# Where the norm's sums, the next weights and the modelled hand-overs stand in three planned feed-forwards

## The chip, the cores and the metric

The kernel runs on one core of a Trainium2 chip. The metric is the time of one execution in microseconds (us) of the device, from which the median of several runs is taken. The core's engines are TensorE (PE in the profile, with its weight loads as PEld), VectorE (DVE), ScalarE (ACT), GpSimd (POOL) and SyncE (SP), which issues most transfers.

## The reference

A decoder trunk of two layers on 512 tokens of width 1024, everything in float32. Cut to what matters:

```
D, F = 1024, 2816
def swiglu_ffn(x, w_gate, w_up, w_down):
    return (jax.nn.silu(x @ w_gate) * (x @ w_up)) @ w_down
for layer in range(2):
    h = h + 0.5 * swiglu_ffn(rms_norm(h, ffn1_norm[layer]), ...)
    u = rms_norm(h, mix_norm[layer])
    h = h + (conformer_conv(u, ...) if layer == 0 else attention(u @ w_q, k_shared, v_shared) @ w_o)
    h = h + 0.5 * swiglu_ffn(rms_norm(h, ffn2_norm[layer]), ...)
    if layer == 0:
        k_shared, v_shared = split(rms_norm(h, kv_norm) @ w_kv)
return rms_norm(h, final_norm)
```

So there are four feed-forwards, each behind an RMS norm, whose factor is one number for each token: the root of the mean square over the 1024 channels.

## The kernel before, in words

**Layout.** Activations stand transposed: 8 chunks of 128 channels by 512 tokens. A weight tile is 128x1024. Each float32 operand is split into a high part (`whi`, `xhi`, `hhi`, made by ScalarE) and the rest (`wlo`, `xlo`, `hlo`, made by VectorE), and a product takes three matmuls: high by high, high by low, low by high (`mm3`, L355 to L357).

**Order of the stages.** Feed-forward 0 and the convolution of layer 0, then feed-forward 1, feed-forward 2, keys, queries and attention, and last feed-forward 3. The first feed-forward is written in program order (`ffn`). Feed-forwards 1, 2 and 3 go through `planned` (L511), and these three are what the change touches.

**The planner.** `planned` writes down every step with an engine, an estimated duration and a rank (`plan.add`), and `Plan.issue` then runs a list scheduling by these numbers: of the steps that can start, it takes the one that can start first, and of those the one of lowest rank. The result is a fixed instruction order for PE, DVE and ACT; each engine works through its own in order. A step that depends on one of another engine is taken to be startable `LATE` = 0.15 us after it, whichever engines they are.

**A feed-forward's start.** The products use `norm.x`, the chunks with the gain but without the norm's factor; the factor is multiplied in when a result leaves PSUM. The factor is made like this: the squares are summed over the chunks into `norm.acc` (VectorE); `token_sums` (L387) adds over the partitions with eight narrow matmuls into the PSUM tile `ss`; `root` takes the inverse root on VectorE in 14 tiny steps (L617 to L621); the result is spread over the partitions by eight diagonal pieces (L628) and two matmuls (L631), and ScalarE copies the row `rb` to SBUF (L633, tile `r_f`). `seed` (L637) writes three PSUM banks that later hold running sums, with any finite matmul of `norm.x[0]`.

**PSUM.** Of eight banks three are these seeds; five go round between `ss`, the row (`pb`) and the products. In a third of the hidden columns the plain columns come first (`plain`, two products of 24 matmuls), and from column 4 on `seven` computes gate and up together by a seven-product scheme, whose products have 12 matmuls of 256 columns each. Between these products stand ScalarE copies of PSUM (`u`, `g1`, `m5`, `u3`; L722 to L730) that the next product waits for. Columns 4 to 21 are of this kind, 18 in each of the three feed-forwards, 54 in all. VectorE prepares sums of `norm.x` for it (`right_sums`, tiles `xs`, `ts`, `tlo`) and of the weights (`st`, `sl`, `wlo`, `ul`).

**Weights.** `unit` hands out the next weight tile and keeps one more loaded ahead, by `load(rank + 0.4)`: transfer, split on ScalarE, split on VectorE, all behind the steps of rank `rank`, the outputs of the running column among them.

Of the kernel before, what the change touches and what calls it, by code (L numbers as in the profile page):

```python
# [15 lines left out]
D = 1024  # L16
# [65 lines left out]

SEVEN = {i: tuple(range(4, 22)) for i in (1, 2, 3)}

DIRECT = 6
Z_BANKS = 4
AV_BANKS = 2
# [3 lines left out]
class Buf:  # L91


    def __init__(self, kind, make):
        self.kind, self.make, self.ap, self.slot = kind, make, None, None
# [7 lines left out]
class Plan:  # L103
# [5 lines left out]
    LATE = 0.15  # L109
    SELF = {"V": 0.14, "A": 0.1, "G": 0.02}  # L110

    def __init__(self, room):
        self.room, self.steps, self.last = dict(room), [], {}

    def add(self, engine, work, do, r=(), w=(), rank=0, port=False):
        n, after = len(self.steps), set()
        for x in r:
            writer, readers = self.last.setdefault(x, [None, []])
            if writer is not None:
                after.add(writer)  # L120
            readers.append(n)
        for x in w:
            writer, readers = self.last.get(x, [None, []])
            after.update(readers)
            if writer is not None:
                after.add(writer)
            self.last[x] = [n, []]
        after.discard(n)
        bufs = tuple(dict.fromkeys(x for x in (*r, *w) if isinstance(x, Buf)))
        self.steps.append((engine, work, do, after, (rank, n), bufs, port or engine == "G"))  # L130
        return n

    def issue(self):
        steps = self.steps
        first, final = {}, {}
        for n, st in enumerate(steps):
            for x in st[5]:
                first.setdefault(x, n)
                final[x] = n
        waits = [len(st[3]) for st in steps]  # L140
        follow = [[] for _ in steps]
        for n, st in enumerate(steps):
            for m in st[3]:
                follow[m].append(n)
        ends, free = [None] * len(steps), {}
        room = {k: list(range(n)) for k, n in self.room.items()}
        ready = {n: 0.0 for n in range(len(steps)) if not waits[n]}
        freeing, uses = [], {}
        for n, st in enumerate(steps):
            for x in st[5]:  # L150
                uses[x] = uses.get(x, 0) + 1
        order, now, port = [], 0.0, (0.0, None)
        while ready or freeing:
            best = None
            for n, t in ready.items():
                engine = steps[n][0]
                t = max(t, free.get(engine, 0.0), now)
                if steps[n][6] and port[1] != engine:
                    t = max(t, port[0])
                new = [x for x in steps[n][5] if first[x] == n]  # L160
                if any(len(room[x.kind]) < sum(y.kind == x.kind for y in new) for x in new):
                    continue
                key = (t, steps[n][4])
                if best is None or key < best[0]:
                    best = (key, n, new)
            if freeing and (best is None or min(freeing)[0] <= best[0][0]):
                t, _, kind, slot = min(freeing)
                freeing.remove(min(freeing))
                room[kind].append(slot)
                now = max(now, t)  # L170
                continue
            assert best is not None, "no step can be issued"
            (t, _), n, new = best
            engine, work, do, _, _, bufs, ported = steps[n]
            for x in new:
                x.slot = room[x.kind].pop(0)
            ends[n] = t + work
            free[engine] = t + work
            if ported:
                port = (t + work, engine)  # L180
            del ready[n]
            order.append((t, n))
            for x in bufs:
                uses[x] -= 1
                if not uses[x]:
                    freeing.append((ends[n] + self.LATE, len(freeing) + len(order), x.kind, x.slot))
            for m in follow[n]:
                waits[m] -= 1
                if not waits[m]:
                    ready[m] = max(  # L190
                        ends[j] + (self.SELF.get(steps[m][0], 0.0) if steps[j][0] == steps[m][0] else self.LATE)
                        for j in steps[m][3]
                    )
        for _, n in order:
            steps[n][2]()
# [3 lines left out]
def decoder_kernel(ctx, tc, xin, gu, dna, dnb, pw1, pw2, kq, wv, wo, out):  # L199
    nc = tc.nc  # L200
    V, A, G, PE = nc.vector, nc.scalar, nc.gpsimd, nc.tensor
# [306 lines left out]
    def planned(idx, norm, after, early=None, sums=None, late=None, tail=None, ahead=1):  # L508


        with ExitStack() as c:  # L511
# [3 lines left out]
            N2 = T // 2  # L515
            seeds = {x: banks[i][:, :N2] for i, x in enumerate(("u0", "u1", "g1"))}
            plan = Plan({"bank": 5, "raw": 3, "whi": 3, "wlo": 3, "wh1": 1, "wl1": 1, "st": 1, "sh": 1, "sl": 1,
                         "uh": 1, "ul": 1, "sq": 2, "m5": 2, "u3": 2, "tg": 2, "tu": 2, "hhi": 8, "hlo": 8, "-": 99})
            add = plan.add
            halves = [slice(0, N2), slice(N2, T)]  # L520

# [10 lines left out]
            def load(rank):  # L532

                src = next(order, None)
                if src is None:
                    return
                i = count[0]
                count[0] += 1
                if isinstance(src, list):
                    held.append(load_seven(i, src, rank))  # L540
                    return
                n = src.shape[-1]
                full = [tile("raw", f"raw{i}", UNIT, F32, wp), tile("whi", f"whi{i}", UNIT, F32R, wp),
                        tile("wlo", f"wlo{i}", UNIT, F32R, wp)]
                add("D", 3.0, lambda: nc.sync.dma_start(full[0]()[:, :n], src), w=[full[0]], rank=rank)
                f = n / UNIT
                add("A", 0.95 * f, lambda: A.copy(full[1]()[:, :n], full[0]()[:, :n]), r=[full[0]], w=[full[1]], rank=rank)  # L547
                add("V", 1.14 * f, lambda: V.tensor_sub(  # L548
                    full[2]()[:, :n], full[0]()[:, :n], full[1]()[:, :n].bitcast(F32)),
                    r=full[:2], w=[full[2]], rank=rank)  # L550
                held.append((full[1], full[2]))
# [48 lines left out]
            def unit(rank):  # L600

                turn[0] += 1
                while len(held) < 2:
                    n = len(held)
                    load(rank + 0.4)
                    if len(held) == n:
                        break
                return held.pop(0)
# [2 lines left out]
            rb = tp.tile([P, T], F32, name=f"r_{norm.name}", tag="r", bufs=1)  # L611
            small, v = (tp.tile([P, 4], F32, name=f"{x}_{norm.name}", tag=x, bufs=1) for x in ("rs", "v"))
            ss, pb, dg = bank(), bank(), []
            add("PE", 0.5, lambda: token_sums(ss()[:, :4], norm.acc), w=[ss], rank=-2)

            def root():
                V.tensor_scalar_add(v, ss()[:, :4], RMS_EPS)  # L617
# [3 lines left out]
                V.tensor_sub(parts[:, 4:], small, parts[:, :4].bitcast(F32))  # L621
                dg.append(parts)

            add("V", 2.4, root, r=[ss], w=["root"], rank=-2)
            for h in range(2):
                dh = tile("sq", f"dg_{norm.name}_{h}", T, F32R, tp)
                for b in range(4):
# [4 lines left out]
                    r=[dh], w=[pb], rank=-2)  # L632
# [1023 lines left out]
```

## Time and profile before

| what | value |
|---|---|
| median of 3 runs | 1917.21 us (1917.21, 1914.41, 1917.89) |
| the profiled execution itself | 1914.83 us |
| its span, first to last instruction | 1913.0 us |
| mean granted clock of TensorE | 0.992 |
| busy: PE, PEld, DVE, ACT, POOL | 1877.6, 1661.9, 1395.3, 956.1, 280.6 us |

The profile counts an engine as busy while an instruction of it runs. The wait rows say which line of which engine stood idle, which instruction's end let it go on, the total time, how often and the longest. The timeline has one row for each instruction: start, duration, engine, line, tiles, and in brackets the idle time before it. Matmuls overlap in the pipeline, so their own durations are longer than the distance from one start to the next, and it is the distance that counts.

The three entries that are spoken of below are the moments at which feed-forwards 1, 2 and 3 begin: near 553, 907 and 1541 us of the span. They are called the first, second and third entry.

### The profile page before, as it was taken

The page shows a single profiled execution, that of the slowest core. Times are in us where ns is not written, and L with a number is a line of the kernel's source. Part 1 is how long each engine was busy: PE and PEld are TensorE (multiplying, and loading weights), DVE is VectorE, ACT ScalarE, POOL GpSimd, SP SyncE. Part 2 cuts the span into 40 slices and gives each one's busy share as a digit, 9 for nine tenths or more (in the row PEclk, how much of TensorE's full clock was granted, in tenths as well). Part 3 has the DMA queues.
Part 4 walks back from the last instruction along what each step waited for, and adds up shares of the span by engine and source line. Part 5 has one row for each costly group of instructions (what it writes and reads, how often), then busy time and mean ns, then how long its engine had stood idle before and what let it go on. Part 6 is the DMA issues. An engine that isn't in the chain of part 4 may idle for free. (4 is left out here: it accounts for less than half of the span.)

```text
span 1913.0 us, 28433 instructions
## 1 busy us (share of the span) xinstructions
PE 1877.6 (98%) x11037; PEld 1661.9 (87%) x11037; DVE 1395.3 (73%) x2295; ACT 956.1 (50%) x1581; POOL 280.6 (15%) x267
## 2 busy tenths in 40 slices
PE   9999999999999999999999999999999999999997
PEld 7888888878988999898798999988888779899896
DVE  6544534598878679577985967878999689577585
ACT  5424324686554345255452544647777645354353
POOL 0311302089700000000000000004543100000001
PEclk9999999999999999999999999999999999999998
DMA  5756746444422323323242232452223122323232
GB/s 202 255 177 236 270 151 216 158 165 156 142 67 89 112 87 100 121 84 115 78 165 78 100 122 89 125 170 74 86 83 83 56 90 97 123 70 130 84 102 70
DMA packets 74262, 237.95 MB, mean 124 GB/s; under 512 B 8464, under 2 KB 11152, under 8 KB 74128
## 3 DMA queue, kind: packets, MB, share of 16 engines
q1 hardware_dynamic: 65776, 209.41, 32.8%
q10 hardware_dynamic: 8352, 26.74, 3.7%
q8 instruction: 86, 1.41, 0.3%
q14 instruction: 48, 0.39, 0.1%
HBM read 200.46 MB, written 31.46 MB: 121 GB/s over the span
## 5 line engine op out<-in xcount | busy, mean ns | idle before, releaser
L249 ACT CAST whi<-raw 128x1024 fp32r<-128x1024 f32 (+3 forms) x109 | 107.5, 989 | 204.0 <-PE pg L356 112.3
L355 PE MATMUL bank<-hhi,whi 128*128 128x512 f32 x510 | 198.5, 389 | 0.0
L356 PE MATMUL bank<-hlo,whi 128*128 128x512 f32 x510 | 198.5, 389 | 0.0
L357 PE MATMUL bank<-hhi,wlo 128*128 128x512 f32 x510 | 198.4, 389 | 0.0
L547 ACT CAST whi<-raw 128x1024 fp32r<-128x1024 f32 (+1 forms) x93 | 92.8, 998 | 191.8 <-PE bank L356 161.8
L505 ACT CAST whi<-raw 128x1024 fp32r<-128x1024 f32 x108 | 113.1, 1048 | 83.9 <-DMA raw<-in_gu_dram 33.9
L250 DVE TENSOR_TENSOR wlo<-raw,whi 128x1024 fp32r<-128x1024 f32 (+3 forms) x109 | 131.2, 1208 | 25.0 <-ACT whi L249 24.7
L357 PE MATMUL pg<-xhi_f,wlo 128*128 128x512 f32 x352 | 137.0, 390 | 0.6 <-DVE wlo L250 0.5
L355 PE MATMUL pg<-xhi_f,whi 128*128 128x512 f32 x352 | 136.3, 390 | 0.8 <-ACT whi L249 0.8
L356 PE MATMUL pg<-xlo_f,whi 128*128 128x512 f32 x352 | 136.9, 389 | 0.0
L801 DVE SCALAR_TENSOR_TENSOR xpar<-bank,xpar 128x512 f32<-128x512 f32 x69 | 47.7, 691 | 122.1 <-PE bank L357 121.5
L506 DVE TENSOR_TENSOR wlo<-raw,whi 128x1024 fp32r<-128x1024 f32 x108 | 131.7, 1220 | 4.1 <-ACT whi L505 4.1
L684 PE MATMUL bank<-thi,whi 128*128 128x256 f32 x432 | 123.3, 285 | 3.2 <-ACT u L730 2.7
L686 PE MATMUL bank<-thi,sl 128*128 128x256 f32 x432 | 122.6, 284 | 1.6 <-DVE sl L506 1.6
L684 PE MATMUL bank<-thi,sh 128*128 128x256 f32 x432 | 122.5, 283 | 0.0
L686 PE MATMUL bank<-xhi_f,wlo 128*128 128x256 f32 x432 | 122.3, 283 | 0.0
L685 PE MATMUL bank<-xlo_f,whi 128*128 128x256 f32 x432 | 122.2, 283 | 0.0
L686 PE MATMUL bank<-thi,wlo 128*128 128x256 f32 x432 | 122.2, 283 | 0.0
L685 PE MATMUL bank<-tlo,sh 128*128 128x256 f32 x432 | 122.2, 283 | 0.0
L685 PE MATMUL bank<-tlo,whi 128*128 128x256 f32 x432 | 122.2, 283 | 0.0
L684 PE MATMUL bank<-xhi_f,whi 128*128 128x256 f32 x432 | 122.2, 283 | 0.0
L548 DVE TENSOR_TENSOR wlo<-raw,whi 128x1024 fp32r<-128x1024 f32 (+1 forms) x93 | 107.2, 1153 | 18.6 <-ACT whi L547 18.5
(400 smaller groups left out, 5713.6 us busy)
## 6 DMA issues: line engine op xcount, KB each, us to landing
raw<-in_gu_dram SPq DMA_DIRECT2D x174, 512.0 KB, 3.3
raw<-in_dna_dram SPq DMA_DIRECT2D x64, 512.0 KB, 3.9
praw<-in_pw_dram SPq DMA_DIRECT2D x24, 512.0 KB, 4.3
aparth<-phi ACTq DMA_DIRECT2D x24, 512.0 KB, 2.6
apartl<-plo ACTq DMA_DIRECT2D x24, 512.0 KB, 3.8
raw<-in_dnb_dram SPq DMA_DIRECT2D x32, 384.0 KB, 3.3
whi<-aparth SPq DMA_DIRECT2D x21, 512.0 KB, 3.3
wlo<-apartl SPq DMA_DIRECT2D x21, 512.0 KB, 4.3
```

The source lines that it names most:

```text
L249: ins = A.copy(dst_hi, src)
L250: (G if on_pool else V).tensor_sub(dst_lo, src, dst_hi.bitcast(F32))
L355: PE.matmul(ps, w[0], x[0], start=first, stop=False)
L356: PE.matmul(ps, w[0], x[1], start=False, stop=False)
L357: PE.matmul(ps, w[1], x[0], start=False, stop=last)
L505: plan.add("A", a, lambda: A.copy(hi(), src()), r=[src, *r], w=[hi], rank=rank)
L506: plan.add("V", v, lambda: V.tensor_sub(lo(), src(), hi().bitcast(F32)), r=[src, hi, *r], w=[lo, *w], rank=rank)
L547: add("A", 0.95 * f, lambda: A.copy(full[1]()[:, :n], full[0]()[:, :n]), r=[full[0]], w=[full[1]], rank=rank)
L548: add("V", 1.14 * f, lambda: V.tensor_sub(full[2]()[:, :n], full[0]()[:, :n], full[1]()[:, :n].bitcast(F32)), r=full[:2], w=[full[2]], ran ...
L684: PE.matmul(d, a[0], b[0], start=start and q == 0, stop=False, skip_group_check=True)
L685: PE.matmul(d, a[0], b[1], start=False, stop=False, skip_group_check=True)
L686: PE.matmul(d, a[1], b[0], start=False, stop=last_, skip_group_check=True)
```

## The change

It has four parts, all of them numbers and steps of the planner; no instruction of an engine is added or taken away.

1. Two steps that issue nothing are put in front: one takes VectorE for 3.5 us of the model, the other (on an engine of its own, "joint") 5.0 us, and `token_sums` depends on the latter. In the model `token_sums` can therefore start no earlier than about 5 us after the feed-forward begins.
2. The estimated duration of `root` goes from 2.4 to 2.9 us.
3. The next weight tile is ranked at `rank - 0.5` in place of `rank + 0.4`, that is ahead of the outputs of the running column. The copies `u` and `g1` have `rank - 1`, and the copy `m5` has `rank - 0.5`.
4. The planner gets a table of hand-over times by the engine that produces (transfer 1.0, PE 0.35, VectorE 0.2, ScalarE 0.2 us) in place of 0.15 for all. Only `planned` uses it.

```
+LAG = {"D": 1.0, "PE": 0.35, "V": 0.2, "A": 0.2, "-": 0.0}
+HEAD = (3.5, 5.0)
...
-    def __init__(self, room):
-        self.room, self.steps, self.last = dict(room), [], {}
+    def __init__(self, room, lag=None):
+        self.room, self.steps, self.last, self.lag = dict(room), [], {}, lag or {}
...
                     ready[m] = max(
-                        ends[j] + (self.SELF.get(steps[m][0], 0.0) if steps[j][0] == steps[m][0] else self.LATE)
+                        ends[j] + (self.SELF.get(steps[m][0], 0.0) if steps[j][0] == steps[m][0]
+                                   else self.lag.get(steps[j][0], self.LATE))
                         for j in steps[m][3]
                     )
...
-                    load(rank + 0.4)
+                    load(rank - 0.5)
...
-            add("PE", 0.5, lambda: token_sums(ss()[:, :4], norm.acc), w=[ss], rank=-2)
+            add("V", HEAD[0], lambda: None, rank=-9)
+            add("joint", HEAD[1], lambda: None, w=["acc_in"], rank=-9)
+            add("PE", 0.5, lambda: token_sums(ss()[:, :4], norm.acc), r=["acc_in"], w=[ss], rank=-2)
...
-            add("V", 2.4, root, r=[ss], w=["root"], rank=-2)
+            add("V", 2.9, root, r=[ss], w=["root"], rank=-2)
```

The lines move by 4 to 6 with it: `token_sums` is L391 after, `mm3` L359 to L361, `seed` L643, the split of a weight on VectorE L552 (L548 before).

The first place is TensorE at the second entry. `bank1_7` is the last output product of feed-forward 1, `acc_f1_1` the sum of squares, `xhi_f1_1_0` the first chunk of the new input. Before:

```order
L355 MATMUL bank1_7_5095<-hhi1_21_8312,whi138_8457 128x512
L356 MATMUL bank1_7_5095<-hlo1_21_8317,whi138_8457 128x512
L357 MATMUL bank1_7_5095<-hhi1_21_8312,wlo138_8464 128x512
L387 MATMUL bank2_3_8570<-onesD_74,acc_f1_1_5081 128x1 x4
L637 MATMUL bank2_0_8567<-xhi_f1_1_0_8336,onesr_72 128x256
L637 MATMUL bank2_1_8568<-xhi_f1_1_0_8336,onesr_72 128x256
L637 MATMUL bank2_2_8569<-xhi_f1_1_0_8336,onesr_72 128x256
L355 MATMUL bank2_4_8571<-xhi_f1_1_0_8336,whi139_8487 128x512
```

After, the same engine at the end of the first product, 21 matmuls of it behind the seeds:

```order
L359 MATMUL bank2_3_8570<-xhi_f1_1_6_8527,whi139_8486 128x512
L360 MATMUL bank2_3_8570<-xlo_f1_1_6_8534,whi139_8486 128x512
L361 MATMUL bank2_3_8570<-xhi_f1_1_6_8527,wlo139_8494 128x512
L391 MATMUL bank2_4_8571<-onesD_74,acc_f1_1_5081 128x1 x4
L359 MATMUL bank2_3_8570<-xhi_f1_1_7_8544,whi139_8486 128x512
L360 MATMUL bank2_3_8570<-xlo_f1_1_7_8548,whi139_8486 128x512
L361 MATMUL bank2_3_8570<-xhi_f1_1_7_8544,wlo139_8494 128x512
L359 MATMUL bank2_5_8572<-xhi_f1_1_0_8341,whi140_8506 128x512
```

The sums moved from the first place of the feed-forward to behind seven eighths of its first product; the seeds are now first. The other two entries read alike, and in all three the matmuls of the row (`pb`) moved from the second product to the third. Apart from these, TensorE's order differs only in a few products that change places with a neighbour.

At the first entry the chunks come in the order 1, 2, 7, 3, 4, 5, 6, 0, so that the seeds, which read chunk 0, read the last one to be made. TensorE there, after (`pp0_1` is the last product of the convolution):

```order
L361 MATMUL pp0_1_5046<-shi7_4483,wlo88_4873 128x256
L643 MATMUL bank1_0_5088<-xhi_f2_0_0_5072,onesr_72 128x256
L643 MATMUL bank1_1_5089<-xhi_f2_0_0_5072,onesr_72 128x256
L643 MATMUL bank1_2_5090<-xhi_f2_0_0_5072,onesr_72 128x256
L359 MATMUL bank1_3_5091<-xhi_f2_0_1_4889,whi89_4878 128x512
```

Here the chunk that was made last is what TensorE meets first; on ScalarE the instruction ahead of that chunk's (the split of weight 91) is the same as before.

The second place is VectorE at the third entry: the split `wlo226` of the second product's weights, and the root of the norm, which begins with `v_f2_1` and ends with `dp_f2_1`. Before:

```order
L620 CAST dp_f2_1_15254<-rs_f2_1_15221 128x4
L621 TENSOR_TENSOR dp_f2_1_15254<-rs_f2_1_15221,dp_f2_1_15254 128x4
L667 TENSOR_TENSOR ts3_0_15270<-xs3_0_15229 128x256
L667 TENSOR_TENSOR ts3_0_15270<-xs3_1_15236,ts3_0_15270 128x256
L548 TENSOR_TENSOR wlo226_15279<-raw226_15231,whi226_15268 128x1024
```

After:

```order
L439 TENSOR_TENSOR acc_f2_1_14819<-acc_f2_1_14819,sq_f2_1_7_15199 128x512
L659 TENSOR_TENSOR xs3_1_15254<-xhi_f2_1_1_15033,xlo_f2_1_1_15034 128x512
L673 TENSOR_TENSOR ts3_0_15259<-xs3_0_15247 128x256
L552 TENSOR_TENSOR wlo226_15261<-raw226_15228,whi226_15252 128x1024
L623 TENSOR_SCALAR v_f2_1_15222<-bank3_4_15216 128x4
L397 TENSOR_SCALAR rs_f2_1_15221<-v_f2_1_15222 128x4
```

The split went from behind the root to ahead of it. Behind the root, `wlo227` and `wlo228` now come before the diagonal pieces.

The third place is ScalarE at the first `seven` of feed-forward 3 (column 4): the copy of `u0` (`bank3_0`), of `m5` and of `g1` (`bank3_2`), between splits of hidden values (`hhi`) and weights (`whi`, `sh`). Before:

```order
L505 CAST whi234_0_15644<-raw234_0_15614 128x1024
L722 COPY bank3_0_15212<-bank3_3_15215 128x256
L505 CAST hhi3_3_15662<-tu3_3_15639 128x512
L725 COPY m5_3_4_15676<-bank3_6_15218 128x256
L726 COPY bank3_2_15214<-bank3_0_15212 128x256
L505 CAST sh234_15695<-st234_15619 128x1024
L730 COPY u3_3_4_15725<-bank3_0_15212 128x256
```

After:

```order
L580 CAST uh233_15614<-raw233_0_15481 128x512
L728 COPY bank3_0_15212<-bank3_4_15216 128x256
L731 COPY m5_3_4_15667<-bank3_7_15219 128x256
L509 CAST hhi3_3_15669<-tu3_3_15637 128x512
L732 COPY bank3_2_15214<-bank3_0_15212 128x256
L509 CAST whi234_0_15689<-raw234_0_15635 128x1024
L509 CAST sh234_15704<-st234_15652 128x1024
```

The split `whi234_0` went from ahead of the copies to behind the copy of `g1`, and `m5` went ahead of `hhi3_3`.

More of the change, by code (lines that the diff above doesn't have):

```diff
@@ L517, in planned @@
             plan = Plan({"bank": 5, "raw": 3, "whi": 3, "wlo": 3, "wh1": 1, "wl1": 1, "st": 1, "sh": 1, "sl": 1,
-                         "uh": 1, "ul": 1, "sq": 2, "m5": 2, "u3": 2, "tg": 2, "tu": 2, "hhi": 8, "hlo": 8, "-": 99})
+                         "uh": 1, "ul": 1, "sq": 2, "m5": 2, "u3": 2, "tg": 2, "tu": 2, "hhi": 8, "hlo": 8, "-": 99}, lag=LAG)
             add = plan.add
```

## The prediction

> **What bounds the kernel now.** I read the busy times first, then TensorE's waits, then the timeline at the places where the long waits stand. The page's first part:
>
> ```profile
> PE 1877.6 (98%) x11037; PEld 1661.9 (87%) x11037; DVE 1395.3 (73%) x2295; ACT 956.1 (50%) x1581; POOL 280.6 (15%) x267
> ```
>
> TensorE is busy for 98% of the span of 1913.0 us, the next engine for 73%. The change leaves TensorE's instructions as they are, so it can only win what TensorE stands idle, 1913.0 − 1877.6 = 35.4 us, and what it runs at a lower clock. TensorE's waits, longest first (line, what ended the wait: total us, times, longest):
>
> ```profile
> PE bank L387 <- DVE acc_f L435: 6.6, 2, 3.5
> PE pb_out1v L1527 <- ACT dg_out L1518: 4.9, 1, 4.9
> PE bank L387 <- DVE acc_f L774: 3.7, 1, 3.7
> PE bank L684 <- ACT u L730: 2.7, 6, 0.8
> PE bank L686 <- DVE sl L506: 1.6, 3, 0.6
> ```
>
> The largest are `token_sums` (L387) waiting for the sum of squares, once at each entry: 6.6 + 3.7 = 10.3 us. L1527 is the end of the kernel, which the change doesn't touch. The last two rows, nine waits and 4.3 us, are hand-overs among the products of `seven`. The second entry on TensorE's timeline:
>
> ```profile
> 894.63 0.39 PE L357 MATMUL bank<-hhi,wlo 128*128 128x512 f32 x1
> ...
> 906.87 0.39 PE L357 MATMUL bank<-hhi,wlo 128*128 128x512 f32 x1
> 910.94 1.84 PE L387 MATMUL bank<-onesD,acc_f 128*128 128x1 f32 x8 [3.69 <-DVE acc_f L774]
> 912.64 0.99 PE L637 MATMUL bank<-xhi_f,onesr 128*128 128x256 f32 x3
> 913.43 0.63 PE L355 MATMUL bank<-xhi_f,whi 128*128 128x512 f32 x1
> ...
> 915.99 0.53 PE L355 MATMUL bank<-xhi_f,whi 128*128 128x512 f32 x1
> 916.36 0.40 PE L356 MATMUL bank<-xlo_f,whi 128*128 128x512 f32 x1
> ```
>
> From 894.63 to 906.87 lie 54 steps of one matmul: 12.24 / 54 = 0.227 us each, the pace at full clock; a product of 24 takes 5.44 us. The wait costs more than its 3.7 us: behind it the seven matmuls from 913.43 to 915.99 stand 0.43 us apart. TensorE comes out of the wait at about half pace and is back at 916.36.
>
> **The change part by part.**
>
> *The sums behind the first product.* What an entry costs now is the time from the end of the last full-pace matmul to the first one after the slow stretch, less what the same work takes at full pace. The sums at full clock stand in the convolution:
>
> ```profile
> 373.57 0.95 PE L387 MATMUL ss_mix<-onesD,acc_mix 128*128 128x1 f32 x8
> 374.38 0.49 PE L355 MATMUL pa<-xhi_mix,whi 128*128 128x512 f32 x1
> ```
>
> That is 374.38 − 373.57 = 0.81 us. The seeds take 913.43 − 912.64 = 0.79 at half pace, so 0.40 by my estimate at full pace. The second entry: 916.36 − (906.87 + 0.23) = 9.26 us for 0.81 + 0.40 + 7 × 0.227 = 2.80 us of work, so 6.46 us too long. The first and third entry:
>
> ```profile
> 552.63 0.28 PE L357 MATMUL pp<-shi,wlo 128*128 128x256 f32 x1
> 556.45 1.05 PE L387 MATMUL bank<-onesD,acc_f 128*128 128x1 f32 x8 [3.54 <-DVE acc_f L435]
> 557.81 0.57 PE L355 MATMUL bank<-xhi_f,whi 128*128 128x512 f32 x1
> ...
> 561.16 0.45 PE L357 MATMUL bank<-xhi_f,wlo 128*128 128x512 f32 x1
> 561.45 0.40 PE L355 MATMUL bank<-xhi_f,whi 128*128 128x512 f32 x1
> ```
>
> ```profile
> 1540.79 0.39 PE L357 MATMUL po<-oh,wlo 128*128 128x512 f32 x1
> 1544.20 1.74 PE L387 MATMUL bank<-onesD,acc_f 128*128 128x1 f32 x8 [3.02 <-DVE acc_f L435]
> 1545.80 0.99 PE L637 MATMUL bank<-xhi_f,onesr 128*128 128x256 f32 x3
> 1546.58 0.63 PE L355 MATMUL bank<-xhi_f,whi 128*128 128x512 f32 x1
> ...
> 1550.85 0.54 PE L356 MATMUL bank<-xlo_f,whi 128*128 128x512 f32 x1
> 1551.22 0.40 PE L357 MATMUL bank<-xhi_f,wlo 128*128 128x512 f32 x1
> ```
>
> The first has nine slow matmuls and began at about 552.75 (the step of a 256-column matmul is about 0.12): 8.70 − (0.81 + 0.40 + 9 × 0.227) = 5.45 us. The third has eleven: 1551.22 − 1541.02 = 10.20, less 0.81 + 0.40 + 11 × 0.227 = 3.71, gives 6.49 us.
>
> Does the new order recover all of it? At the second and third entry the seeds read chunk 0, which was made long before. The first product needs the last chunk only at its last three matmuls, 0.40 + 4.76 + 0.81 = 6 us after the entry; the sums need `acc` after 5.2 us. `acc` was there at 910.94, that is 3.8 us after the second entry, and 3.2 us after the third. Both arrive in time, so nothing is left to wait for: 6.46 + 6.49. At the first entry the seeds come first and read the last chunk, and ScalarE makes that one behind a weight split:
>
> ```profile
> 552.83 1.04 ACT L249 CAST whi<-raw 128x1024 fp32r<-128x1024 f32 x1 [0.95 <-PE pp L356]
> 553.78 0.72 ACT L421 ACTIVATE xhi_f<-xpar 128x512 fp32r<-128x512 f32 x1
> ```
>
> It ends at 554.50. That order is unchanged, so TensorE still stands from 552.75 to about 554.55, 1.80 us, and recovers 5.45 − 1.80 = 3.65 us, if the clock holds. Sum of the three: 16.6 us.
>
> Whether the clock holds depends on what makes it fall. The clock at the first entry, by slices of 1 us (PE busy, granted clock, transfers):
>
> ```profile
> 557.00:558.00 1.00, 1.00 (x9) 0.93 0.75 303
> 561.00:562.00 1.00, 1.00 (x5) 0.86 0.00 0
> ```
>
> With full and half clock as the two values, the clock fell at 557.86 and rose at 561.28, a stretch of 3.42 us that starts after the wait is over. The shortest wait that was followed by a fall is the third entry's, 1544.20 − 1541.02 = 3.2 us; a wait of 1.80 us is little more than half of it, so I take no fall. The Trainium skill, page "TensorE: Matmul & The Clock Gate", section "Why this matters for your kernels", asks for no gap of TensorE above about 3 us between bursts, and its Part 1 gives a free-running window of about 3.4 us, one idle window of which halves the clock. The stretch of 3.42 us agrees with that window; by that rule the 1.80 us do no harm and the sum is the same, while 3.2 us sufficed at the third entry, so a window need not be wholly idle.
>
> *The root and the row.* At the second entry the sums now end at 907.10 + 0.40 + 4.76 + 0.81 = 913.07, against 910.94 + 1.84 = 912.78 before. So the row comes when it came, while TensorE is 6.5 us further on:
>
> ```profile
> 923.55 0.69 DVE L752 TENSOR_TENSOR tg<-bank,r_f 128x512 f32<-128x512 f32 x1 [0.16 <-ACT r_f L633]
> ```
>
> TensorE's cover are the free banks: the fourth product, at 907.10 + 0.40 + 0.81 + 3 × 5.44 + 0.5 for the row's own matmuls = 925.1, takes the bank of the sums, the fifth (930.5) that of the row, and only the sixth (936.0) needs one that this `tg` step and its like empty, from 924.2 on. Cost zero; without that cover each us of delay would count once for each entry.
>
> *Next weights first.* With the first product 5 to 6 us earlier, the second product's weights are due earlier. At the third entry the order now has `wlo226` ahead of the root. The rows of before:
>
> ```profile
> 1544.09 0.69 DVE L653 TENSOR_TENSOR xs<-xhi_f,xlo_f 128x512 f32<-128x512 f32 x1
> 1549.42 1.22 DVE L548 TENSOR_TENSOR wlo<-raw,whi 128x1024 fp32r<-128x1024 f32 x1
> ```
>
> In the new place it starts one 0.4 us step behind `xs`, at about 1545.2, and is done at 1546.4; TensorE needs it at 1541.02 + 0.40 + 0.81 + 5.44 + 0.45 = 1548.1. In the old place, done at 1550.6, it would have cost 2.5 us. In SyncE's queue this part changes only feed-forward 2, where weight loads move ahead of stores of the shared key and value input; nothing of the following columns reads those.
>
> *Hand-over times.* The nine waits of 4.3 us are what a planner with 0.15 us for every hand-over leaves. Bounds: all of it goes, or as much again is added by the new order. I take half of it gone, 2.2 us, since the waits are of the two kinds that the change re-ranks and re-times.
>
> *Sum.* 16.6 + 2.2 = 18.8 us. The profiled execution took 1914.83 us, so 1896.0. The median of the runs lies 2.4 us above the profiled one; I leave that distance as it is: 1917.21 − 18.8 = 1898.4.
>
> **Rivals.**
>
> *The clock falls at the first entry after all.* For it speaks that a fall doesn't need a whole idle window. Price: at least nine matmuls at 0.42 in place of 0.227 us, 1.7 us; at most the eleven-matmul stretch and slow sums of the third entry, 10.20 − 3.18 − 3.71 = 3.3 us. Then 1900.1 to 1901.7. Chance 0.15.
>
> *VectorE becomes the bound before the first `seven`.* It has a fixed load between an entry and the first product of column 4, and that stretch gets shorter:
>
> ```profile
> 907.10:958.82 51.72, 48.03 (x206) 39.93 (x206) 47.12 (x92) 20.54 (x29) 0.00 (x0) 0.93 0.26 88
> 950.05 1.22 DVE L506 TENSOR_TENSOR wlo<-raw,whi 128x1024 fp32r<-128x1024 f32 x1
> 951.18 1.22 DVE L506 TENSOR_TENSOR sl<-st,sh 128x1024 fp32r<-128x1024 f32 x1
> 956.59 0.68 DVE L577 TENSOR_TENSOR ul<-raw,uh 128x512 fp32r<-128x512 f32 x1
> ```
>
> VectorE is busy for 47.12 of 51.72 us; after the change 45.3 us remain, 1.9 too few. Against it: column 4 now begins at 958.82 − 6.46 = 952.4; `wlo` was done at 951.3 and `sl`, needed a product later, at 952.4, so even an unmoved VectorE is just in time, and the work that is too much is for later columns. Price 1.9 us for each of the second and third entry, 3.8 together: 1902.2. Chance 0.08.
>
> *Slower: the re-ranked weight splits get in front of hand-overs.* ScalarE's copies stand between products of each `seven`; a weight split (1.04 us, above) that starts just ahead of one makes TensorE wait. The six waits for `u` cost 2.7 / 6 = 0.45 us each. If every one of the 54 columns got one, that would be 24.3 us against 16.6: 7.7 us slower, 1924.9. It decides from 16.6 / 0.45 = 37 columns on. Against it: the copies `u` and `g1` keep a lower rank than the loads, and at column 4 of feed-forward 3 the weight split moved behind the copies, not ahead of them. Chance 0.03; a weaker form that eats most of the gain, 0.02.
>
> That the change does not do what it says is excluded by the order: the sums stand behind 21 matmuls of the first product in all three.
>
> **How the numbers follow.** Forecast 0.72, the rivals 0.15, 0.08, 0.03 and 0.02. The time is the forecast's, 1898. The low end is the profiled time less 16.6 and all of the 4.3 us: 1893.9, so 1893.5; the high end is the median less 16.6 and with the first two rivals' 3.3 and 1.9: 1905.8, so 1905.5. About 0.2% of the time, 3.8 us, is what a measurement can tell from no change: faster 0.95, same 0.02, slower 0.03.
>
> **What would show it.** In the profile after: no wait row of `token_sums` for `acc_f`; one wait of about 1.8 us of the seeds for `xhi_f` near 554; matmuls 0.23 us apart right after the second and third entry; `sl` and `u` waits of some 2 us in all; a mean granted clock above 0.992. I am wrong if the seeds or the first product wait at the later entries, if TensorE waits at column 4, or if waits for `u` number in the dozens.

## The result, and the profile after

The changed kernel takes 1893.24 us (median of 1892.80, 1894.13, 1893.14 and 1893.35), against 1916.12 us of the kernel before beside it. The ratio is 0.9881, 95% interval 0.9864 to 0.9898: 22.9 us or 1.2% faster. The forecast was 1898.0 us with a range from 1893.5: the sign is right, the gain is 4 us larger than forecast, and the time lies just below the range.

The first part of the page after:

```profile
PE 1867.3 (99%) x11035; PEld 1655.7 (88%) x11037; DVE 1392.4 (74%) x2295; ACT 956.6 (51%) x1581; POOL 281.1 (15%) x267
```

TensorE is busy for 10.3 us less with the same instructions, and the span of 1891.1 us is 21.9 us shorter. The other half, 11.6 us, was idle time. The mean granted clock rose from 0.992 to 0.997. Line numbers are 4 to 6 higher now (`token_sums` is L391, the seeds L643, the products of `seven` L690 to L692). TensorE's waits after, with only the rows that belong to the three feed-forwards and the end:

```profile
PE pb_out1v L1533 <- ACT dg_out L1524: 4.9, 1, 4.9
PE bank L643 <- ACT xhi_f L425: 1.6, 1, 1.6
...
PE bank L690 <- ACT bank L732: 0.6, 1, 0.6
...
PE bank L359 <- ACT whi L551: 0.5, 1, 0.5
...
PE bank L690 <- ACT u L736: 0.3, 1, 0.3
```

The rows of `token_sums` for `acc_f` (10.3 us) are gone. Of the hand-over waits in `seven`, two small ones are left (0.9 us); the kernel before had ten (4.8 us), the nine that the prediction counts and this one:

```profile
PE bank L684 <- ACT bank L726: 0.5, 1, 0.5
```

The row of L359 in the profile after was not foreseen. Where the time went, stage by stage: each row runs from the last matmul ahead of an entry to the first product of `seven`, or from there to the end of the feed-forward. First the kernel before (length, PE busy, and near the end PE's granted clock):

```profile
552.63:603.45 50.82, 47.28 (x209) 38.98 (x207) 45.39 (x89) 21.63 (x29) 0.00 (x0) 0.97 0.25 83
603.45:906.87 303.42, 301.78 (x2041) 280.58 (x2039) 223.52 (x341) 139.42 (x216) 0.00 (x0) 1.00 0.30 100
906.87:958.82 51.95, 48.27 (x207) 39.93 (x206) 47.35 (x92) 20.77 (x29) 0.00 (x0) 0.93 0.26 90
958.82:1262.26 303.44, 302.12 (x2041) 280.77 (x2040) 233.67 (x356) 146.37 (x227) 4.43 (x7) 1.00 0.36 120
1540.79:1592.81 52.02, 49.00 (x208) 40.39 (x206) 44.66 (x86) 21.54 (x29) 0.00 (x0) 0.93 0.25 81
1592.81:1885.37 292.56, 290.69 (x1987) 270.77 (x1986) 214.01 (x327) 130.62 (x203) 0.00 (x0) 1.00 0.30 98
```

The same stretches after:

```profile
552.35:599.76 47.41, 45.77 (x209) 37.84 (x207) 43.17 (x86) 20.48 (x28) 0.00 (x0) 1.00 0.22 68
599.76:902.16 302.40, 301.82 (x2040) 280.60 (x2039) 225.38 (x344) 140.68 (x217) 0.00 (x0) 1.00 0.31 104
902.16:947.76 45.60, 45.60 (x208) 37.85 (x206) 43.69 (x87) 20.36 (x29) 0.00 (x0) 1.00 0.24 84
947.76:1248.94 301.18, 301.18 (x2041) 280.52 (x2040) 236.10 (x361) 146.69 (x227) 4.83 (x7) 1.00 0.37 124
1527.41:1573.76 46.35, 45.83 (x207) 37.91 (x206) 42.82 (x84) 21.59 (x29) 0.00 (x0) 1.00 0.25 80
1573.76:1863.43 289.67, 289.41 (x1988) 270.56 (x1986) 215.20 (x330) 131.09 (x203) 0.00 (x0) 1.00 0.30 101
```

The entries give 50.82 − 47.41 = 3.41, then 6.35 and 5.67 us, 15.4 together; the rest of the feed-forwards gives 1.02 + 2.26 + 2.89 = 6.2 us, almost all of it in the products of `seven` (see the last column of the table below). What lies outside these rows moved by 0.3 us. The second entry, where TensorE has no idle time left and the clock is whole; the sums stand behind the first 21 matmuls:

```profile
902.16 0.40 PE L361 MATMUL bank<-hhi,wlo 128*128 128x512 f32 x1
902.40 0.52 PE L643 MATMUL bank<-xhi_f,onesr 128*128 128x256 f32 x3
902.75 0.40 PE L359 MATMUL bank<-xhi_f,whi 128*128 128x512 f32 x1
...
907.30 0.39 PE L361 MATMUL bank<-xhi_f,wlo 128*128 128x512 f32 x1
907.53 0.95 PE L391 MATMUL bank<-onesD,acc_f 128*128 128x1 f32 x8
908.34 0.49 PE L359 MATMUL bank<-xhi_f,whi 128*128 128x512 f32 x1
```

At the first entry the foreseen wait of the seeds for chunk 0 is there, and the products behind it run at full pace:

```profile
554.27 0.62 PE L643 MATMUL bank<-xhi_f,onesr 128*128 128x256 f32 x3 [1.64 <-ACT xhi_f L425]
554.73 0.39 PE L359 MATMUL bank<-xhi_f,whi 128*128 128x512 f32 x1
554.96 0.40 PE L360 MATMUL bank<-xlo_f,whi 128*128 128x512 f32 x1
```

The theory after the result is this. The moved sums give the entries' 15.4 us by themselves; the ranks and the hand-over times together give the 6.2 us in the products of `seven`; and these two add. The rivals: the moved sums need the re-ranked loads to pay (the third entry's weights), or one of the two planner settings does nothing.

### The profile page after: what moved, and what is told of

Its sections match the earlier page's. It is cut to its first block, busy times and chain, and to the rows that moved or that the text cites. A ratio compares the mean times of both kernels' runs of the same rounds, so it can differ in the third digit from the quotient of the medians.

```text
span 1891.1 us, 28503 instructions
## 1 busy us (share of the span) xinstructions
PE 1867.3 (99%) x11035; PEld 1655.7 (88%) x11037; DVE 1392.4 (74%) x2295; ACT 956.6 (51%) x1581; POOL 281.1 (15%) x267
## 4 chain that ended last, share of the span: by engine, by line
PE 92%; DVE 3%; ACT 2%; POOL 1%; issue 1%; DMA 1%; POOLq 0%; DVEq 0%; ACTq 0%
PE bank L690 9%; PE bank L691 9%; PE bank L692 9%; PE bank L359 8%; PE bank L360 8%; PE bank L361 8%; PE pg L361 4%; PE pg L359 4%; PE pg L360 4%; PE pd L359 2%; PE pd L361 2%; PE pd L360 2%; PE z L1374 2%; PE pa L359 1%; PE pa L361 1%; PE pa L360 1%
## 5 line engine op out<-in xcount | busy, mean ns | idle before, releaser
L359 PE MATMUL bank<-hhi,whi 128*128 128x512 f32 x510 | 198.5, 389 | 0.0
L361 PE MATMUL bank<-hhi,wlo 128*128 128x512 f32 x510 | 198.4, 389 | 0.0
L551 ACT CAST whi<-raw 128x1024 fp32r<-128x1024 f32 (+1 forms) x93 | 92.8, 998 | 183.3 <-PE bank L360 168.1
L361 PE MATMUL pg<-xhi_f,wlo 128*128 128x512 f32 x352 | 137.1, 390 | 0.5 <-DVE wlo L254 0.4
L359 PE MATMUL pg<-xhi_f,whi 128*128 128x512 f32 x352 | 136.2, 390 | 1.1 <-ACT whi L253 1.1
L690 PE MATMUL bank<-thi,whi 128*128 128x256 f32 x432 | 122.6, 284 | 0.8 <-ACT bank L732 0.6
L690 PE MATMUL bank<-thi,sh 128*128 128x256 f32 x432 | 122.5, 283 | 0.0
L692 PE MATMUL bank<-xhi_f,wlo 128*128 128x256 f32 x432 | 122.5, 283 | 0.0
L692 PE MATMUL bank<-thi,sl 128*128 128x256 f32 x432 | 122.2, 283 | 0.0
L692 PE MATMUL bank<-thi,wlo 128*128 128x256 f32 x432 | 122.2, 283 | 0.0
L690 PE MATMUL bank<-xhi_f,whi 128*128 128x256 f32 x432 | 122.2, 283 | 0.0
L552 DVE TENSOR_TENSOR wlo<-raw,whi 128x1024 fp32r<-128x1024 f32 (+1 forms) x93 | 107.2, 1153 | 14.0 <-ACT whi L551 13.9
```

What stands on the lines that cost most here:

```text
L359: PE.matmul(ps, w[0], x[0], start=first, stop=False)
L361: PE.matmul(ps, w[1], x[0], start=False, stop=last)
L552: add("V", 1.14 * f, lambda: V.tensor_sub(full[2]()[:, :n], full[0]()[:, :n], full[1]()[:, :n].bitcast(F32)), r=full[:2], w=[full[2]], ran ...
L690: PE.matmul(d, a[0], b[0], start=start and q == 0, stop=False, skip_group_check=True)
L692: PE.matmul(d, a[1], b[0], start=False, stop=last_, skip_group_check=True)
```

## The experiments

**Which part gives what.** The change has three switches: the sums moved (H, with the planner's new time for the root), the loads re-ranked (R), the hand-over times (L). The two kernels of the record are none and all; the other six combinations were run.

`head_only` is the kernel before with H alone; `rank_only`, `lag_only` and `rank_lag` leave H out. As edits of the changed kernel:

```
# without L
-"hhi": 8, "hlo": 8, "-": 99}, lag=LAG)
+"hhi": 8, "hlo": 8, "-": 99})
# without R
-                    load(rank - 0.5)
+                    load(rank + 0.4)
# without H
-            add("V", HEAD[0], lambda: None, rank=-9)
-            add("joint", HEAD[1], lambda: None, w=["acc_in"], rank=-9)
-            add("PE", 0.5, ..., r=["acc_in"], w=[ss], rank=-2)
+            add("PE", 0.5, ..., w=[ss], rank=-2)
-            add("V", 2.9, root, r=[ss], w=["root"], rank=-2)
+            add("V", 2.4, root, r=[ss], w=["root"], rank=-2)
```

> The kernel before with the sums behind the first product alone (weight loads at rank +0.4, every hand-over 0.15 us). Theory A, the parts add: the entries give their 15.4 us alone (landmarks from the last full-pace matmul of the entry to the first product of `seven`: -3.4, -6.3, -5.7), the rest of the feed-forwards stays as before, so 1900.5 to 1901.5 us and a ratio of 0.992. Theory B, the head needs the re-ranked loads: at the third entry the second product waits for its weights, a matmul of line 360 or 361 with an idle of about 2.5 us near 1536, and copies and splits of `seven` wait more often than before, so 1903.5 or more.

> The kernel before with the weight loads at rank -0.5 alone. The three waits of products for `sl` (1.6 us listed, 1.6 + 3 x 0.26 = 2.4 us of pace) should go if the re-ranked loads are what ends them. Theory A: 1.5 to 3 us faster, 1913 to 1914.5. Theory B, that splits of weights now stand ahead of copies between products: as many u and g1 waits as before or more, 1916 or slower.

> The kernel before with the planner's hand-over times alone. Theory A: the six waits for `u` (2.7 us listed, about 4.3 us of pace) go, and those for `sl` stay: 3 to 5 us faster, 1911 to 1913. Theory B: longer hand-overs only move the steps, the u waits stay: 1916 within 1 us.

> Loads at rank -0.5 and the hand-over times, sums as in the kernel before. Theory A: the entries stay as before, the rest of the feed-forwards gives its 6.2 us, so 1909.5 to 1910.5, the sum of what the two give alone. Theory B: the rest of the feed-forwards gets its 6.2 us only with the sums moved, because the slow matmuls behind each entry shift the plan: under 3 us, 1913 or more.

> The changed kernel without the hand-over times. From the four runs so far (sums moved alone -14.9 us, ranks alone -5.5, hand-over times alone +4.9, ranks and hand-over times -8.8 against before). Theory A, sums and ranks add: 1915.7 - 14.9 - 5.5 = 1895.3, and the re-ranked loads also take away the 2.6 us that the sums alone lose in the products of `seven`: 1893 to 1895.5. Theory B, the hand-over times are what pays once loads are re-ranked (the step from ranks alone to ranks and hand-over times is 3.3 us): 1896.5 or more.

> The changed kernel with the weight loads at rank +0.4. Theory A, hand-over times without the re-ranked loads make more waits in `seven` (excess over the pace 14.2 us alone, against 8.5 before and 1.3 with both): 1900.7 + 4.9 = 1905.6, between 1903 and 1908, with an excess over 10 us in `seven`. Theory B, the sums moved change the plan enough that the hand-over times pay without the ranks too: 1898 or less.

Measured. "Lost in `seven`" is worked out from each timeline: the sum, over neighbouring 256-column matmuls, of the distance of their starts less the full pace of 0.12 us.

| kernel | median, us | before beside it | difference | ratio, 95% interval | lost in `seven`, us |
|---|---|---|---|---|---|
| before | | | | | 8.5 |
| head_only (H) | 1900.74 | 1915.67 | −14.9 | 0.9924 [0.9911, 0.9937] | 11.2 |
| rank_only (R) | 1910.18 | 1915.67 | −5.5 | 0.9970 [0.9959, 0.9982] | 3.6 |
| lag_only (L) | 1920.60 | 1915.67 | +4.9 | 1.0027 [1.0016, 1.0039] | 14.2 |
| rank_lag (R, L) | 1906.89 | 1915.67 | −8.8 | 0.9953 [0.9940, 0.9966] | 1.3 |
| head_rank (H, R) | 1896.25 | 1915.73 | −19.5 | 0.9897 [0.9883, 0.9910] | 5.6 |
| head_lag (H, L) | 1905.56 | 1915.73 | −10.2 | 0.9945 [0.9932, 0.9957] | 14.2 |
| the change (H, R, L) | 1893.24 | 1916.12 | −22.9 | 0.9881 [0.9864, 0.9898] | 2.2 |

H adds to whatever else is there: −14.9 on nothing, −14.0 on R, −15.1 on L, −14.1 on both. R and L do not add: −5.5 and +4.9 alone, −8.8 together. L costs 4.7 to 4.9 us as long as the loads have the old rank, and gives 3.3 to 3.4 us once they have the new one. (The last row's kernel before is 0.4 us above the others'; by the kernels' own medians H gives −13.7 on both, and L gives 3.0 us on H and R.) Of the expectations for the first four runs only theory A of `head_only` held, by its time. `rank_only` and `rank_lag` gained 2.8 and 2.6 us more than their theories A allowed, and `lag_only` was slower than either of its theories. Of the two expectations for `head_rank` neither fits as written (1896.25 lies just under the second's 1896.5): H and R nearly add, and L still pays 3.4 us. For `head_lag` the first holds, to within 0.1 us.

The rival with the third entry's weights falls. With the old rank `head_only` has the third entry as short as the change, 46.35 us:

```profile
1530.93:1577.28 46.35, 45.83 (x208) 37.92 (x207) 41.97 (x83) 21.59 (x29) 0.00 (x0) 1.00 0.25 80
1577.28:1872.11 294.83, 290.88 (x1988) 270.80 (x1986) 216.04 (x330) 130.80 (x203) 0.00 (x0) 1.00 0.31 99
```

and VectorE has the second product's `wlo` there ahead of the root, which moved behind the sums:

```profile
1534.85 1.22 DVE L552 TENSOR_TENSOR wlo<-raw,whi 128x1024 fp32r<-128x1024 f32 x1
1538.03 0.16 DVE L623 TENSOR_SCALAR v_f<-bank 128x4 f32<-128x4 f32 x1 [1.97 <-PE bank L391]
```

What H alone loses lies in the second of the stretches: 294.83 against 289.67 us after and 292.56 before. R's part is seen in the waits. Of `seven` these rows are left with H alone, and one of 0.2 us:

```profile
PE bank L690 <- ACT u L736: 3.6, 5, 1.0
...
PE bank L692 <- DVE sl L510: 1.3, 3, 0.6
...
PE bank L690 <- ACT bank L732: 1.2, 1, 1.2
```

Those for `sl` are weights that come late; with R alone no row for `sl` is left. For L without R this is TensorE at one column of `lag_only`:

```profile
740.25 0.28 PE L690 MATMUL bank<-xhi_f,wlo 128*128 128x256 f32 x1
740.98 0.38 PE L688 MATMUL bank<-xhi_f,whi 128*128 128x256 f32 x1 [0.45 <-ACT bank L726]
...
742.51 0.28 PE L688 MATMUL bank<-thi,sh 128*128 128x256 f32 x1
...
745.27 0.28 PE L690 MATMUL bank<-thi,sl 128*128 128x256 f32 x1
746.00 0.38 PE L688 MATMUL bank<-thi,whi 128*128 128x256 f32 x1 [0.45 <-ACT bank L730]
```

The product at 740.98 stands directly behind the one whose bank ScalarE first copies (L726), and the one at 746.00 directly behind the second such copy (L730). The products `s1` and `s2` of the weights' sums, which the kernel before has between the first pair, come only at 742.51 and after, so the product that covers the second pair is used up. My reading is that a planner that believes hand-overs to be long, but has its loads in the last rank, takes `s1` for late and runs the product of the same bank first. Which of L's numbers does that was asked by one more run, `lag_only` with the transfers' time back at the old 0.15 us:

```
-LAG = {"D": 1.0, "PE": 0.35, "V": 0.2, "A": 0.2, "-": 0.0}
+LAG = {"D": 0.15, "PE": 0.35, "V": 0.2, "A": 0.2, "-": 0.0}
```

> The run `lag_only` (4.9 us slower than before, with 14.2 us lost in the products of `seven` against 8.5) with the hand-over time of a transfer back at 0.15 us, the engines' times as in the change. Theory A, the transfers' 1.0 us is what hurts without the re-ranked loads, since it lets the planner put splits of weights later: no slower than before, 1915.7 or less, and an excess of 8.5 us or less in `seven`. Theory B, TensorE's 0.35 us is what hurts: 1919 to 1921, excess of 13 us or more. In between: both do.

It took 1922.30 us beside 1916.42, ratio 1.0031 [1.0019, 1.0043], and lost 15.7 us in `seven`. So the transfers' time is not what hurts, and the engines' times are: theory B, with a time 1.3 us above its range. Of those only PE's (0.35) is much larger than the old 0.15; that PE's alone does it wasn't tried.

**What still waits at the entries.** `seeds` lets the seeds read the chunk that was made first. What they write is overwritten by ScalarE's copies before it counts. `seeds_banks` reverses the planner's five banks as well, and `seeds_after` puts the seeds behind the first product, with the sums:

```
# seeds
-PE.matmul(x, onesr, norm.x[0][0][:, :N2], start=True, stop=True)
+PE.matmul(x, onesr, norm.x[norm.order[0]][0][:, :N2], start=True, stop=True)
# seeds_banks: that, and
-b = Buf("bank", lambda: banks[3 + b.slot])
+b = Buf("bank", lambda: banks[7 - b.slot])
# seeds_after: of the changed kernel only
-add("PE", 0.4, seed, w=list(seeds), rank=-2)
+add("PE", 0.4, seed, r=["acc_in"], w=list(seeds), rank=-2)
```

> The changed kernel, its seeds reading the chunk that was made first instead of chunk 0. Only the first entry changes, where the seeds wait 1.64 us for chunk 0. Theory A: the first product's bank is the one that the last pointwise column stood in (bank 5 in both), and VectorE reads that column until about 0.75 us after the entry, so 0.4 to 0.6 us of wait are left there: 1.1 to 1.4 us faster, 1892. Theory B: no wait is left, 1.9 us faster (1.64 and the 0.26 us that a wait adds to the pace), 1891.3. Theory C: the product waits for something else that chunk 0 hid, 1893.

> As the run before, and the planner's five banks in reverse order, so that the first product of a feed-forward takes a bank that nothing read lately. Theory A: the wait at the third entry (listed as 0.52 us for a weight cast) was VectorE's read of the last output column in the same bank; it goes, and so does what is left at the first: 0.9 to 1.3 us faster than the run before, 1890.5 to 1891. Theory B: the cast that the profile names is the cause: the third entry's wait stays, and no more than 0.5 us is won over the run before.

> The changed kernel with the seeds, too, behind the first product (they wait for the same step as the sums), so that they neither wait for chunk 0 nor take the first bank. Reversing the planner's list of banks changed nothing in the program's banks: a bank gets its place by the order of first use, and the first product came fourth, in bank 5, which is the last column's. With the first product first it gets bank 0. Theory A, the bank is the cause (VectorE still reads the last column from it): the waits of 0.40 us at the first and 0.52 us at the third entry go, the first product follows the last matmul at the pace at all three, about 1.2 us faster than the run `seeds`, 1889.6 us. Theory B, the weight cast that the profile names is the cause: the wait of 0.5 us at the third entry stays, 1890.2 to 1890.8.

`seeds` took 1890.77 us (0.9867 [0.9852, 0.9882]), 2.5 us less than the change by the medians. By the time that would be theory B or better, but the profile shows theory A: at the first entry its stretch is 46.20 against 47.41 us, 1.2 us less, with the foreseen rest of a wait:

```profile
553.53 0.50 PE L359 MATMUL bank<-xhi_f,whi 128*128 128x512 f32 x1 [0.40 <-DVE xpar L1224]
```

Of the rest, 0.9 us lie in the rest of feed-forward 1 (301.46 against 302.40 us), where the change's wait of 0.6 us for L732 is gone; why it went wasn't followed up. `seeds_banks` took 1891.06 us, no different: the waits stayed. But it tried nothing, since reversing the list changes no bank. In the built program a bank gets its place by the order of first use, and the first product stands in bank 5 in both kernels. `seeds_after` gives it bank 0. (The bank numbers are read from the program; a trace doesn't show them.) It took 1889.53 us (0.9865 [0.9848, 0.9881]), 1.2 us under `seeds`, and all three entries are without a gap (last matmul ahead of the entry to the first product of `seven`):

```profile
552.41:597.85 45.44, 45.44 (x209) 37.78 (x207) 43.06 (x86) 20.31 (x28) 0.00 (x0) 1.00 0.22 71
899.79:945.32 45.53, 45.53 (x208) 37.85 (x207) 43.70 (x87) 20.42 (x29) 0.00 (x0) 1.00 0.24 84
1525.39:1570.91 45.52, 45.52 (x208) 37.85 (x206) 42.84 (x84) 21.64 (x29) 0.00 (x0) 1.00 0.24 82
```

So the wait that the profile of the change puts down to a weight cast (L551) was for VectorE's last read of the same bank. The row of VectorE in the change:

```profile
1527.85 0.69 DVE L1459 TENSOR_TENSOR xpar<-po,xpar 128x512 f32<-128x512 f32 x1 [2.02 <-PE po L361]
```

It ends at 1528.54, the cast at 1528.66, and TensorE starts at 1528.69: by the times alone either could be it. In `seeds_after` the first product starts just after the cast does, without waiting for its end, so the cast is not what it needs:

```profile
1525.59 1.06 ACT L551 CAST whi<-raw 128x1024 fp32r<-128x1024 f32 x1 [2.64 <-PE po L360]
1525.61 0.39 PE L359 MATMUL bank<-xhi_f,whi 128*128 128x512 f32 x1
```

The version with `seeds_after` is the fastest run here; against the change it is 3.7 us by the medians, and 1.97 + 0.07 + 0.83 = 2.9 us by the entries' stretches.

**What a wait of the sums costs.** `head12` and `head05` put the sums behind 6 and 3 matmuls of the first product instead of 21 or 24, so that a wait of chosen length comes back:

```
-HEAD = (3.5, 5.0)
+HEAD = (3.5, 1.2)   # head12
+HEAD = (3.5, 0.5)   # head05
```

> The changed kernel with the sums behind 6 matmuls of the first product instead of 21 to 24, so that they wait again: `acc` comes 3.9 us after the second entry, the sums are due 1.9 us after it, a wait of 2.0 us; 0.65 us at the third, none at the first. Theory A, only waits of about 3 us lower the clock: the time grows by the waits alone, 2.7 to 3.0 us, to 1896, and matmuls stay 0.23 us apart. Theory B, 2 us suffice: at the second entry 8 matmuls or more 0.42 us apart, 1.7 to 3.3 us more, 1898 to 1899.5.

> The same with the sums behind 3 matmuls: waits of 0.7, 2.7 and 1.4 us at the three entries. Theory A: the time grows by the waits, 4.8 to 5.2 us, to 1898.3, matmuls 0.23 us apart. Theory B, 2.7 us in a stretch of 3.4 us is idle enough: the clock falls at the second entry, 1.7 to 3.3 us more, 1900 to 1901.6.

`head12` took 1896.70 us (0.9902 [0.9887, 0.9917]) and `head05` 1901.06 (0.9926 [0.9912, 0.9941]). The waits came as worked out, and at the second entry of `head12` 1.95 us were enough to lower the clock:

```profile
905.90 1.02 PE L391 MATMUL bank<-onesD,acc_f 128*128 128x1 f32 x8 [1.95 <-DVE acc_f L780]
906.78 0.47 PE L359 MATMUL bank<-xhi_f,whi 128*128 128x512 f32 x1
907.10 0.46 PE L360 MATMUL bank<-xlo_f,whi 128*128 128x512 f32 x1
907.36 0.63 PE L361 MATMUL bank<-xhi_f,wlo 128*128 128x512 f32 x1
907.79 0.63 PE L359 MATMUL bank<-xhi_f,whi 128*128 128x512 f32 x1
```

The matmuls from 907.36 on stand 0.43 us apart, and the granted clock of the same kernel in slices of 1 us (third column from the end) is 0.64 here, then 0.50, and 0.66 on the way back:

```profile
907.00:908.00 1.00, 1.00 (x4) 0.79 (x4) 0.83 (x6) 0.00 (x0) 0.00 (x0) 0.64 0.00 0
...
910.00:911.00 1.00, 1.00 (x5) 0.79 (x4) 1.00 (x3) 0.00 (x0) 0.00 (x0) 0.66 0.00 0
```

With full and half clock as the two values that is a stretch of 3.4 us again. The entry's stretch is 49.37 us against 45.60 in the change: 2.1 us without a matmul, and 1.6 us for some eight matmuls at 0.43 in place of 0.23 us. Theory A holds for `head12` by its time (1896) and falls by its mechanism. In `head05` both the first entry (1.64 us for the seeds, then 0.6 for the sums) and the second (2.63 us) lost the clock, and theory B is right there.

## Why the prediction was right or wrong

**Where the bound lies.** Right: only TensorE's idle time and its clock were to be had, and both came.

**The entries.** Forecast 6.46 + 6.49 + 3.65 = 16.6 us, measured 6.35 + 5.67 + 3.41 = 15.4. The mechanism is as described at the first two, with the seeds' wait of 1.64 us listed at the first; at the third one wait came in addition. The third is 0.8 us smaller because the first product then waited for its bank (0.52 us listed), a wait that `token_sums` had covered before: "nothing is left to wait for" was one wait short.

**Hand-over times.** This is the step that failed, by its size: "I take half of it gone, 2.2 us", with 4.3 us as the most. The rest of the feed-forwards gave 6.2 us, which is 4.0 us more and the largest error of the sum. The bound itself was wrong, because it added up idle times of the wait rows. A row counts from the modelled end of the matmul ahead, which lies 0.16 us behind the moment when the next could have started. One of the waits of before:

```profile
861.74 0.28 PE L686 MATMUL bank<-xhi_f,ul 128*128 128x256 f32 x1
862.81 0.39 PE L684 MATMUL bank<-thi,whi 128*128 128x256 f32 x1 [0.79 <-ACT u L730]
863.03 0.28 PE L685 MATMUL bank<-tlo,whi 128*128 128x256 f32 x1
```

Listed are 0.79 us. From start to start it is 1.07 where the pace is 0.12, and the next distance is 0.22: 0.95 + 0.10 = 1.05 us lost. Added up like this, `seven` lost 8.5 us before and 2.2 after, which is the 6.2 us to within 0.1. Of the 8.5 us the prediction saw 4.3 in its nine rows; 0.5 are the tenth row, 2.9 what the rows leave out of their own waits, and 0.8 shorter waits that have no row. The same working on the entries went by starts and was right to 1.2 us.

**Next weights first.** Wrong in its only price: "In the old place, done at 1550.6, it would have cost 2.5 us". I took the old place as fixed, but the root moves with the sums, and `head_only` has `wlo` ahead of it without any new rank. The part pays elsewhere: 4.6 us on top of H, and 12.7 us on top of H and L.

**The distance of the profiled run from the median.** "I leave that distance as it is": 2.4 us, from three runs. The kernel before, run 39 times more beside the experiments, had medians of 1915.7, 1915.7, 1915.8 and 1916.4 us, 0.8 to 1.6 us above its profile, and single runs from 1911.05 to 1919.76; after the change the distance is 0.4 us and the four runs lie within 1.3. Part of this scatter the change removes. At the first entry the clock stays low for 3.4 us in the profile of before and for 6.8 us in those of `rank_only`, `lag_only` and `rank_lag`, whose first stretch is 52.45 us instead of 50.82 (`lag_no_dma` has 50.82 again). The third stretch, too, has two lengths: 52.02 us in before and 50.38 in `lag_no_dma`. So a run can differ from the next by 1.6 us at an entry. Before's profile had the shorter length at the first entry and the longer at the third; why it lies below the median is not shown. Of the error of 5.2 us against the forecast of the text (1898.4), 2.0 come from this distance and 3.1 from the terms above: +4.0 hand-overs, −1.2 entries, +0.3 elsewhere.

**The cover of the root and the row.** Right: no product behind the sums waits for a bank at any entry, and VectorE's load, 43.69 of 45.60 us at the second, did not show up as a wait at column 4.

**The rivals.** The clock held at the first entry, as forecast, but the argument for it was wrong, that the shortest wait with a fall behind it was 3.2 us and 1.80 us "little more than half" of that. 1.95 us of idle lowered the clock in `head12`, and 1.64 + 0.6 us in `head05`. The trace of before already spoke against it. With full and half clock as the two values, the clock fell at 909.44 at the second entry, 2.3 us after TensorE could have gone on (907.10) and before the wait was over; the granted clock is the third column from the end:

```profile
909.00:910.00 1.00, 0.00 (x0) 0.00 (x0) 0.81 (x2) 0.93 (x2) 0.00 (x0) 0.72 0.00 0
```

And at the end of the attention it fell at 1520.42, where none of the five waits since 1515 is longer than 1.32 us; together they are 2.9 us:

```profile
1519.90 0.80 PE L355 MATMUL po<-oh,whi 128*128 128x512 f32 x2 [1.32 <-ACT oh L249]
1520.00:1521.00 1.00, 1.00 (x3) 0.57 (x4) 0.57 (x1) 0.00 (x0) 0.00 (x0) 0.71 0.00 0
```

So the forecast of no fall came true by a smaller margin than its argument gave, and in that it was lucky. The Trainium skill, page "TensorE: Matmul & The Clock Gate", section "Why this matters for your kernels", which the prediction cites behind that argument, asks for no gap above about 3 us; the runs here don't agree, since 1.95 us sufficed, and the measurement decides. The slower rival has a relative in `lag_only`, 4.9 us slower, though by the order of products and not by splits ahead of copies.

## What to carry to other kernels

Price a wait by the distance of starts on TensorE's timeline, less the pace, and not by the idle time of its row: here the rows of `seven` fell by 3.9 us and the time by 6.2. A reduction that only scales results belongs behind the first products, and once it is moved, look at what it covered: the bank of the last tile and the seeds were next, worth another 3.7 us by the medians. Planner settings are to be tried together and apart, since one alone (L) can lose 4.9 us and yet give 3.4 us once another (R) is in place.

## What the runs showed of the hardware

A wait of 1.95 us lowered TensorE's clock to half for 3.4 us (`head12`). One of 1.64 us at the first entry did not, in the change and in the four other profiles that have it alone (`head_only`, `head_rank`, `head_lag`, `head12`). Waits near each other seem to count together: 1.64 and 0.6 us in `head05`, and five waits of 0.17 to 1.32 us, 2.9 us within 5 us, in the attention of the kernel before. The change leaves this last fall in place (granted clock 0.56 in the slice from 1506 to 1507 us of the profile after), so what it costs is still to be had.

At the entries the clock stays low for about 3.4 or 6.8 us. The same wait of 3.5 us at the first entry was followed by 3.4 us in the kernel before and by 6.8 us in `rank_only`. So at this kernel a wait of 2 to 3 us can cost nearly double its length, and the same wait 1.6 us more in one run than in another. What decides between the two lengths was not followed up.
